# Norm and rotation of q and k: the squares in two buffers, the product with the cosines on VectorE

## The chip, the core and the metric

One NeuronCore of a Trainium2 chip runs the whole program; nothing is shared with other cores. The metric is the device time of one launch in microseconds (us), as the median of three runs. A core has engines with instruction queues of their own, each worked off in order: TensorE (PE in the rows; its weight loads are PEld), VectorE (DVE), ScalarE (ACT), GpSimd (POOL) and SyncE (SP), which here only issues transfers.

## The reference

One layer of a hybrid network on 1024 tokens of width 1024, all in float32: a feed-forward block, then a mixer of two branches (a recurrence, RWKV-7, and a dilated attention), then a second feed-forward block and a gated embedding. The change touches the attention's preparation of q and k:

```python
def rms_norm(x, gain):
    y = x * lax.rsqrt(jnp.mean(x * x, axis=-1, keepdims=True) + RMS_EPS)
    return y * gain
def apply_rope(x, cos, sin):
    x1, x2 = jnp.split(x, 2, axis=-1)
    return jnp.concatenate([x1 * cos - x2 * sin, x2 * cos + x1 * sin], axis=-1)
def dilated_attention_mix(z, cos, sin, q_gain, k_gain):
    q, k, v = jnp.split(z, 3, axis=-1)          # 12 heads of 64, in three groups of 4
    q = apply_rope(rms_norm(q, q_gain), cos, sin)
    k = apply_rope(rms_norm(k, k_gain), cos, sin)
    for gi, (window, dilation) in enumerate(((128, 1), (512, 4), (2048, 16))):
        ...   # banded causal attention of the group's 4 heads, with the log-sum-exp of each row
    ...       # the three groups' outputs, weighted by a softmax over their log-sum-exps
```

## The kernel before

Products of float32 matrices are made from split operands: a number is a rounded high part and a low part, and `mm3` issues three matmuls (L266 to L268) for each product. A weight tile is loaded by SyncE (L258), ScalarE writes its high part (L250) and GpSimd its low part (L251, tile `wsp`).

After the recurrence, from about 1387 us of the span to 1700, several streams are woven into one program:

- `qkv_gemm` makes q, k and v of groups 1 and 2 (g = 1, 2), 128 tokens at a time, in a PSUM tile `g` (two buffers) that ScalarE copies to `raw` (L1433). Group 0 was made earlier and is read back from memory into the tiles `ot` (L1491, two buffers). A gate product (L1352) shares the `g` buffers.
- `qk_post` is the norm and rotation. It runs 12 times: three groups, and in each q and k for two halves of 512 tokens (n = 0 to 3). Each time ScalarE squares the 128x1024 tile (L1510, into `rt2`), VectorE sums the squares over the 64 columns of a head (L1513), makes one over the root with eleven instructions on 128x16 numbers (L238 to L244), and rotates: a product with the cosines (L1512, into `rt1`, two buffers), two half products with the sines (L1519, L1520, into `rt3`), their sum (L1524) and the scaling (L1526). TensorE then transposes the result (L1531) and ScalarE copies it to `qkT`. Before the change GpSimd makes the product with the cosines, and `rt2` has one buffer, so a second square waits until L1513 has read the first.
- `attn_core` goes through eight blocks of queries in each group: scores on TensorE (L1591, tile `s`), mask and maximum on VectorE (L1595, then L1599), exponentials on ScalarE (L1601), transposes (L1613), copies (L1615 on VectorE, L1617 on ScalarE), and the product with v (L1634).
- `branch_r` is the recurrence's output product, which fills TensorE where the others leave room.

The order in which an engine's instructions stand is not the text's order: the streams yield at marked places with estimated times, and the layer that records the program places each engine's instructions by estimates of its own. Once built, an engine's order is fixed, and an instruction that waits holds back all that stand behind it. In the rows digits are left out of a tile's name: `rt1`, `rt2` and `rt3` all read `rt` there.

Of the kernel before, what the change touches and what calls it, by code (L numbers as in the profile page):

```python
# [13 lines left out]
ALU = mybir.AluOpType  # L14
# [4 lines left out]
P = 128  # L19
# [152 lines left out]
class K:  # L172
# [1307 lines left out]
    def qk_post(self, sp, sp1, pp, rawD, env):  # L1480

        nc = self.nc
        V, A, G, PE = nc.vector, nc.scalar, nc.gpsimd, nc.tensor
        done = env["done"]
        for g in range(NG):
            yield lambda: g < 2 or ("core", g - 2) in done
            tr = [self.t(sp, [P, 2, T], f"qkT{qk}", bufs=2) for qk in range(2)]

            def load0(n):
                t = self.t(sp1, [P, T], f"ot{n % 2}").rearrange("p (i h d) -> p i h d", i=4, h=4)  # L1490
                nc.sync.dma_start(t.rearrange("p i h d -> p i (h d)"), rawD[n % 2, :, n // 2 * 4:n // 2 * 4 + 4])  # L1491
                return t

            if g == 0:
                r0 = [load0(0), load0(1)]
                yield 0, 6.0
            for n in range(4):
                qk, hf = (n % 2, n // 2) if g == 0 else (n // 2, n % 2)
                Ct, St = self.rt[qk]
                if g == 0:  # L1500
                    raw = r0[n]
                else:
                    yield lambda: (g, qk, hf) in env["raw"]
                    raw = env["raw"][g, qk, hf]
                yield 0, 0.6
                isl = slice(hf * 4, hf * 4 + 4)
                bc = lambda t, o, n: t[:, isl, None, o:o + n].to_broadcast([P, 4, 4, n])
                ss = self.t(self.hp, [P, 4, 4], "ass", bufs=2)
                sq = self.t(sp, [P, 4, 4, 64], "rt2")
                A.activation(sq, raw, AF.Square)  # L1510
                t1 = self.t(sp, [P, 4, 4, 64], "rt1", bufs=2)
                G.tensor_tensor(out=t1, in0=raw, in1=bc(Ct, 0, 64), op=ALU.mult)  # L1512
                V.tensor_reduce(out=ss, in_=sq, axis=AX.X, op=ALU.add)  # L1513
                V.tensor_scalar(out=ss, in0=ss, scalar1=1.0 / 64, scalar2=1e-6, op0=ALU.mult, op1=ALU.add)
                yield 0, 1.5
                rs = self.rsqrt(sp, ss, "ars")
                yield 0, 1.0
                t2 = self.t(sp, [P, 4, 4, 64], "rt3")
                V.tensor_tensor(out=t2[:, :, :, 0:32], in0=raw[:, :, :, 32:64], in1=bc(St, 0, 32), op=ALU.mult)  # L1519
                V.tensor_tensor(out=t2[:, :, :, 32:64], in0=raw[:, :, :, 0:32], in1=bc(St, 32, 32), op=ALU.mult)  # L1520
                if g == 0 and n < 2:
                    r0.append(load0(n + 2))
                yield 0, 1.0
                V.tensor_tensor(out=t1, in0=t1, in1=t2, op=ALU.add)  # L1524
                yield 0, 1.0
                V.tensor_tensor(out=t1, in0=t1, in1=rs[:, :, :, None].to_broadcast([P, 4, 4, 64]), op=ALU.mult)  # L1526
                yield 0, 5.0
                for pr in range(2):
                    ps = self.t(pp, [P, HALF], "pt", bufs=2)
                    for i in range(4):  # L1530
                        PE.transpose(ps[:, i * P:(i + 1) * P], t1[:, i, 2 * pr:2 * pr + 2].rearrange("p h d -> p (h d)"),  # L1531
                                     self.ident)
                    t = tr[qk][:, pr]
                    if g == 0:
                        A.activation(t[:, hf * HALF:(hf + 1) * HALF], ps, AF.Copy)
                    elif g == 1:
                        A.activation(t.rearrange("p (r h l) -> p r h l", r=4, h=2)[:, :, hf],
                                     ps.rearrange("p (l r) -> p r l", r=4), AF.Copy)
                    else:
                        A.activation(t.rearrange("p (j h m) -> p j h m", j=8, h=2)[:, :, hf],  # L1540
                                     ps.rearrange("p (m j) -> p j m", j=8), AF.Copy)
                    yield 0.43, 0
                done.add(("post", g, qk, hf))
                env["qk"][g] = tr
# [569 lines left out]
```

## Time and profile before

| | |
|---|---|
| runs | 2688.59, 2697.83, 2698.99 us; median 2697.83 |
| profiled execution | 2694.29 us, its span (first to last instruction) 2692.5 |
| busy, share of the span | TensorE 93%, VectorE 60%, GpSimd 42%, ScalarE 36% |
| mean granted clock of TensorE | 0.964 of full speed |

The span is the time that the rows count from its start. Busy shares are averages over stages that have different limits; the rows further down are taken from the stage that the change touches. The chain of work that ended last runs 46% of the span through TensorE and 12% through VectorE.

### The profile page before, as it was taken

The page shows a single profiled execution, that of the slowest core. Times are in us where ns is not written, and L with a number is a line of the kernel's source. Part 1 is how long each engine was busy: PE and PEld are TensorE (multiplying, and loading weights), DVE is VectorE, ACT ScalarE, POOL GpSimd, SP SyncE. Part 2 cuts the span into 40 slices and gives each one's busy share as a digit, 9 for nine tenths or more (in the row PEclk, how much of TensorE's full clock was granted, in tenths as well). Part 3 has the DMA queues.
Part 4 walks back from the last instruction along what each step waited for, and adds up shares of the span by engine and source line. Part 5 has one row for each costly group of instructions (what it writes and reads, how often), then busy time and mean ns, then how long its engine had stood idle before and what let it go on. Part 6 is the DMA issues. An engine that isn't in the chain of part 4 may idle for free.

```text
span 2692.5 us, 36600 instructions
## 1 busy us (share of the span) xinstructions
PE 2492.6 (93%) x14285; PEld 2040.2 (76%) x14285; DVE 1623.3 (60%) x2591; ACT 977.2 (36%) x1700; POOL 1142.7 (42%) x637
## 2 busy tenths in 40 slices
PE   6899999899899999999989999879799999999889
PEld 5688888677787677779876988558578888778677
DVE  5855555898724565555456345462775556698952
ACT  6333333334444333333324354222533333333441
POOL 3675555544525233332222121240666555554540
PEclk9899999999999999999997999889899999999999
DMA  5322222646343222222231012661132222463432
GB/s 197 94 89 68 94 79 94 229 165 204 115 142 88 61 77 70 71 69 69 77 125 32 32 48 87 174 227 55 55 102 82 75 89 84 156 231 120 160 118 92
DMA packets 272497, 289.16 MB, mean 107 GB/s; under 512 B 46282, under 2 KB 202540, under 8 KB 272068
## 3 DMA queue, kind: packets, MB, share of 16 engines
q1 hardware_dynamic: 264932, 274.59, 31.2%
q10 hardware_dynamic: 7392, 12.23, 1.3%
q8 instruction: 112, 1.84, 0.3%
q14 instruction: 61, 0.50, 0.1%
HBM read 222.64 MB, written 64.14 MB: 107 GB/s over the span
## 4 chain that ended last, share of the span: by engine, by line
PE 46%; DVE 12%; issue 4%; POOL 3%; DMA 3%; ACT 2%; SPq 0%; DVEq 0%; POOLq 0%; ACTq 0%
PE g L266 7%; PE g L268 6%; PE g L267 6%; PE dn L267 5%; PE dn L268 5%; PE dn L266 5%; POOL wsp L251 2%; PE tr L268 1%; PE tr L267 1%; PE tr L266 1%; DVE X L1126 1%; DVE sub L1124 1%; PE s L1591 1%; PE t L1060 1%; DMA wr<-ffn_w_down 1%
## 5 line engine op out<-in xcount | busy, mean ns | idle before, releaser
L251 POOL TENSOR_TENSOR wsp<-wr,wsp 128x1024 fp32r<-128x1024 f32 (+1 forms) x158 | 356.6, 2263 | 378.8 <-ACT wsp L250 338.5
L251 POOL TENSOR_TENSOR wsp<-wst,wsp 128x1024 fp32r<-128x1024 f32 x71 | 176.1, 2483 | 344.9 <-ACT wsp L250 189.3
L251 POOL TENSOR_TENSOR wsp<-ws,wsp 128x1024 fp32r<-128x1024 f32 x88 | 221.1, 2514 | 214.5 <-ACT wsp L250 212.0
L266 PE MATMUL g<-wsp,h 128*128 128x256 f32 (+1 forms) x664 | 213.9, 322 | 19.5 <-ACT raw L1433 9.8
L266 PE MATMUL g<-h,wsp 128*128 128x512 f32 x496 | 215.9, 435 | 13.6 <-DVE h L1730 8.6
L268 PE MATMUL g<-wsp,h 128*128 128x256 f32 (+1 forms) x664 | 207.1, 312 | 0.0
L267 PE MATMUL g<-wsp,h 128*128 128x256 f32 (+1 forms) x664 | 206.0, 310 | 0.7 <-POOL wsp L251 0.7
L268 PE MATMUL g<-h,wsp 128*128 128x512 f32 x496 | 200.6, 405 | 2.1 <-POOL wsp L251 2.1
L267 PE MATMUL g<-h,wsp 128*128 128x512 f32 x496 | 200.6, 404 | 0.0
L408 DVE TENSOR_TENSOR ws<-wr 128x512 f32<-128x512 f32 x56 | 86.3, 1550 | 171.8 <-POOL x L251 170.4
L250 ACT ACTIVATE wsp<-wr 128x1024 fp32r<-128x1024 f32 (+1 forms) x158 | 134.3, 853 | 134.4 <-PE g L268 63.4
L250 ACT ACTIVATE wsp<-ws 128x1024 fp32r<-128x1024 f32 (+1 forms) x110 | 106.4, 968 | 202.1 <-PE dn L268 78.4
L266 PEld LDWEIGHTS g<-wsp,h 128*128 128x128 f32 x664 | 137.0, 206 | 29.6 <-ACT raw L1433 10.7
L266 PE MATMUL dn<-wsp,h 128*128 128x512 f32 x360 | 144.3, 402 | 6.5 <-DVE x L793 6.4
L267 PE MATMUL dn<-wsp,h 128*128 128x512 f32 x360 | 144.0, 400 | 6.5 <-POOL wsp L251 6.5
L268 PE MATMUL dn<-wsp,h 128*128 128x512 f32 x360 | 143.1, 399 | 0.8 <-DVE h L251 0.6
L267 PEld LDWEIGHTS g<-wsp,h 128*128 128x128 f32 x664 | 136.9, 206 | 4.9 <-POOL wsp L251 0.9
L268 PEld LDWEIGHTS g<-wsp,h 128*128 128x128 f32 x664 | 136.9, 206 | 4.6 <-issue 1.0
L464 DVE TENSOR_TENSOR act<-act,m 128x512 f32<-128x512 f32 x88 | 129.3, 1469 | 1.4
L266 PEld LDWEIGHTS g<-h,wsp 128*128 128x128 f32 x496 | 96.4, 194 | 38.5 <-DVE h L1730 9.5
L268 PE MATMUL dn<-h,wsp 128*128 128x512 f32 x320 | 124.6, 389 | 0.0
L266 PE MATMUL dn<-h,wsp 128*128 128x512 f32 x320 | 124.5, 389 | 0.0
(469 smaller groups left out, 6673.5 us busy)
## 6 DMA issues: line engine op xcount, KB each, us to landing
wr<-ffn_w_down SPq DMA_DIRECT2D x44, 1024.0 KB
wst<-w_in SPq DMA_DIRECT2D x60, 512.0 KB
wr<-ffn_w_gate SPq DMA_DIRECT2D x44, 512.0 KB
wr<-ffn_w_up SPq DMA_DIRECT2D x44, 512.0 KB
actD<-act SPq DMA_DIRECT2D x44, 512.0 KB
a<-actD SPq DMA_DIRECT2D x12, 1024.0 KB
gate<-gst SPq DMA_DIRECT2D x26, 256.0 KB
wst<-ffn_w_down SPq DMA_DIRECT2D x10, 512.0 KB
```

What stands on the lines that cost most here:

```text
L250: nc.scalar.activation(dst[:, 0], src, AF.Copy)
L251: (lo_eng or nc.vector).tensor_tensor(out=dst[:, 1], in0=src, in1=dst[:, 0].bitcast(F32), op=ALU.subtract)
L266: mm(ps, lhsT=l[0], rhs=r[0], start=first, stop=False)
L267: mm(ps, lhsT=l[0], rhs=r[1], start=False, stop=False)
L268: mm(ps, lhsT=l[1], rhs=r[0], start=False, stop=last)
L408: self.nc.vector.tensor_tensor(out=out, in0=R[:, i], in1=R[:, j], op=op)
L464: eng.tensor_tensor(out=a, in0=a, in1=v, op=ALU.mult)
L1060: PE.matmul(psd[h][:, i2, e].rearrange("p (a s) -> p a s", a=2), lhsT=BK[hr, i, 2 * e:2 * e + 2].rearrange("p a s -> p (a s)"), rhs=QR[hr, ...
L1124: V.tensor_tensor(out=pr[:, :s + 1, :n], in0=XT[:, :s + 1, s:s + 1].to_broadcast([64, s + 1, n]), in1=at[:, s:s + 1, s + 1:].to_broadcast( ...
L1126: V.tensor_tensor(out=XT[:, :s + 1, s + 1:], in0=XT[:, :s + 1, s + 1:], in1=pr[:, :s + 1, :n], op=ALU.subtract)
L1591: PE.matmul(ps[h][:, pr, :nk * P], lhsT=qT[hr, pr, j * P:(j + 1) * P], rhs=kT[hr, pr, k0:k0 + nk * P], start=True, stop=True)
```

## The change

Two lines of `qk_post` change. The squares get a second buffer, and the product with the cosines is issued on VectorE:

```diff
                 ss = self.t(self.hp, [P, 4, 4], "ass", bufs=2)
-                sq = self.t(sp, [P, 4, 4, 64], "rt2")
+                sq = self.t(sp, [P, 4, 4, 64], "rt2", bufs=2)
                 A.activation(sq, raw, AF.Square)
                 t1 = self.t(sp, [P, 4, 4, 64], "rt1", bufs=2)
-                G.tensor_tensor(out=t1, in0=raw, in1=bc(Ct, 0, 64), op=ALU.mult)
+                V.tensor_tensor(out=t1, in0=raw, in1=bc(Ct, 0, 64), op=ALU.mult)
                 V.tensor_reduce(out=ss, in_=sq, axis=AX.X, op=ALU.add)
```

GpSimd loses 12 instructions, VectorE gains 12; SyncE's order is the same as before. Around them the order on TensorE, VectorE and ScalarE shifts between the end of the recurrence and the norm of the last tile. Three places follow, as differences (+ only now, - only before).

ScalarE at the start of the attention: the squares of group 0's four tiles (rt 1842, 1857, 1877, 1910 for n = 0 to 3), the copies of `raw`, the gate's copy and a weight's high part.

```order
 L1510 ACTIVATE rt_1842_11915<-ot_1831_11828 128x1024
+L1510 ACTIVATE rt_1857_12073<-ot_1832_11830 128x1024
 L1352 ACTIVATE gst_1819_11776<-g_11777 128x512
 L250 ACTIVATE wsp_12129<-wst_12127 128x1024
-L1510 ACTIVATE rt_1857_12073<-ot_1832_11830 128x1024
+L1510 ACTIVATE rt_1877_12207<-ot_1848_11970 128x1024
 L1433 ACTIVATE raw_11842<-g_11869 128x256
-L1510 ACTIVATE rt_1877_12207<-ot_1848_11970 128x1024
 L1433 ACTIVATE raw_11842<-g_11895 128x256
```

The second square now stands directly behind the first, ahead of the gate's copy (L1352). The third stands ahead of both copies of `raw` (L1433); before, the first of these stood between the second square and the third.

VectorE at the same place: rt 1843 and 1858 are the products with the cosines for n = 0 and 1, rt 1847 and 1861 those with the sines, rt 1842 and 1857 the squares.

```order
+L1512 TENSOR_TENSOR rt_1843_11917<-ot_1831_11828,rope_1824_11816 128x1024
 L1519 TENSOR_TENSOR rt_1847_11967<-ot_1831_11828,rope_1825_11817 128x16x32
 L1520 TENSOR_TENSOR rt_1847_11967<-ot_1831_11828,rope_1825_11817 128x16x32
+L1512 TENSOR_TENSOR rt_1858_12075<-ot_1832_11830,rope_1826_11820 128x1024
 L1524 TENSOR_TENSOR rt_1843_11917<-rt_1843_11917,rt_1847_11967 128x1024
 L1519 TENSOR_TENSOR rt_1861_12117<-ot_1832_11830,rope_1827_11821 128x16x32
+L1513 TENSOR_REDUCE ass_11914<-rt_1842_11915 128x16
+L1513 TENSOR_REDUCE ass_12072<-rt_1857_12073 128x16
+L1514 TENSOR_SCALAR ass_11914<-ass_11914 128x16
 L1520 TENSOR_TENSOR rt_1861_12117<-ot_1832_11830,rope_1827_11821 128x16x32
+L238 TENSOR_SCALAR arsy_11941<-ass_11914 128x16
+L1514 TENSOR_SCALAR ass_12072<-ass_12072 128x16
```

Both products stand in VectorE's line, and the sums of squares of n = 0 and n = 1 (L1513) follow behind one L1524; before, the first stood behind both.

VectorE in the middle of group 0's attention: rt 1927 and 1964 are the products for the first two tiles of group 1, and S 12413 is the fifth block of scores of group 0.

```order
+L1512 TENSOR_TENSOR rt_1927_12447<-raw_11842,rope_1824_11816 128x1024
 L1524 TENSOR_TENSOR rt_1927_12447<-rt_1927_12447,rt_1939_12504 128x1024
+L1615 COPY PT_12363<-pt_12370 128x512
 L1526 TENSOR_TENSOR rt_1927_12447<-rt_1927_12447,arsy_12481 128x1024
-L1615 COPY PT_12363<-pt_12370 128x512
+L1512 TENSOR_TENSOR rt_1964_12637<-raw_11972,rope_1824_11816 128x1024
+L1595 ISA S_12413,ast_12185<-s_12414,cst_a_11814 128x256
+L1595 ISA ast_12185 128x1
```

The two products stand ahead of the mask and maximum of a block of scores, and each waits there for transposes (L1531) that free its buffer of `rt1`, as GpSimd waited before.

## Rows read from the trace of the kernel before

**Rows 1.** Busy time by stage: attention's start, and what follows.
```profile
core 0: us, PE busy (x) PEld busy (x) DVE busy (x) ACT busy (x) POOL busy (x), PEclk, DMA share, GB/s
1387.00:1480.00 93.00, 77.23 (x450) 59.10 (x449) 69.62 (x174) 37.21 (x93) 27.96 (x10) 0.80 0.18 60
1480.00:1560.00 80.00, 79.93 (x493) 76.72 (x492) 28.55 (x69) 24.95 (x59) 13.22 (x5) 1.00 0.08 27
```

**Rows 2.** TensorE's timeline, rows that waited (idle time and releaser in brackets).
```profile
1401.52 0.58 PE L266 MATMUL g<-wsp,h 128*128 128x256 f32 x1 [9.36 <-ACT raw L1433]
...
1433.37 1.13 PE L1591 MATMUL s<-qkT,qkT 64*128 64x256 f32 x6 [1.51 <-DVE ast L1595]
...
1435.54 0.48 PE L1613 MATMUL pt<-cst_p,S 128*128 128x128 f32 x1 [1.04 <-ACT S L1601]
...
1462.37 2.76 PE L1591 MATMUL s<-qkT,qkT 64*128 64x256 f32 x8 [2.28 <-DVE ast L1595]
...
1593.18 0.44 PE L1613 MATMUL pt<-cst_p,S 128*128 128x128 f32 x2 [1.99 <-ACT S L1601]
...
1618.55 1.94 PE L1531 MATMUL pt<-cst_p,rt 128*128 128x128 f32 x8 [5.93 <-DVE rt L1526]
```

**Rows 3.** Busy time in stretches of 2 us, columns as in Rows 1.
```profile
1434.00:1436.00 2.00, 0.96 (x7) 0.34 (x4) 2.00 (x5) 1.01 (x5) 0.00 (x0) 0.83 0.02 6
...
1462.00:1464.00 2.00, 1.63 (x6) 1.43 (x7) 2.00 (x8) 0.00 (x0) 0.00 (x0) 0.66 0.00 0
...
1476.00:1478.00 2.00, 2.00 (x14) 1.33 (x12) 0.77 (x2) 0.90 (x2) 0.00 (x0) 0.93 0.00 0
...
1592.00:1594.00 2.00, 0.82 (x7) 0.81 (x8) 1.76 (x10) 1.48 (x6) 0.00 (x0) 1.00 0.00 0
```

**Rows 4.** VectorE's timeline in the first stall (start, duration, instruction).
```profile
1388.12 2.87 DVE L1520 TENSOR_TENSOR rt<-ot,rope 128x512 f32<-128x512 f32 x1
...
1391.10 3.21 DVE L1524 TENSOR_TENSOR rt<-rt,rt 128x1024 f32<-128x1024 f32 x1
...
1394.34 2.71 DVE L1519 TENSOR_TENSOR rt<-ot,rope 128x512 f32<-128x512 f32 x1
...
1398.90 1.21 DVE L1513 TENSOR_REDUCE ass<-rt 128x16 f32<-128x1024 f32 x1
```

**Rows 5.** ScalarE's and GpSimd's timelines in the first stall.
```profile
1400.14 1.06 ACT L1510 ACTIVATE rt<-ot 128x1024 f32<-128x1024 f32 x1 [10.21 <-DVE ass L1513]
...
1387.55 5.67 POOL L1512 TENSOR_TENSOR rt<-ot,rope 128x1024 f32<-128x1024 f32 x2 [13.69 <-DMA ot<-raw]
...
1393.19 3.31 POOL L251 TENSOR_TENSOR wsp<-wst,wsp 128x1024 fp32r<-128x1024 f32 x1
```

**Rows 6.** Lines of the norm: count, duration ns min/median/max, first and last start.
```profile
L1524 DVE TENSOR_TENSOR rt<-rt,rt x12: 1208/1224/3241, 1391.1 to 1643.3; 128x1024 f32<-128x1024 f32 x12
...
L1520 DVE TENSOR_TENSOR rt<-raw,rope x8: 677/2870/2896, 1435.5 to 1640.3; 128x512 f32<-128x512 f32 x8
...
L1513 DVE TENSOR_REDUCE ass<-rt x12: 1205/1208/1212, 1398.9 to 1646.4; 128x16 f32<-128x1024 f32 x12
...
L1512 POOL TENSOR_TENSOR rt<-raw,rope x8: 2391/2848/2912, 1453.1 to 1639.8; 128x1024 f32<-128x1024 f32 x8
```

**Rows 7.** VectorE's timeline ahead of the wait that ends at 1462.37.
```profile
1455.54 1.23 DVE L1524 TENSOR_TENSOR rt<-rt,rt 128x1024 f32<-128x1024 f32 x1 [3.90 <-POOL rt L1512]
...
1458.54 1.73 DVE L238 TENSOR_SCALAR arsy<-ass 128x16 int32<-128x16 int32 x1
```

**Rows 8.** VectorE's and GpSimd's timelines ahead of the wait that ends at 1618.55.
```profile
1605.08 2.26 DVE L1519 TENSOR_TENSOR rt<-raw,rope 128x512 f32<-128x512 f32 x1 [8.56 <-ACT raw L1433]
...
1610.27 3.24 DVE L1524 TENSOR_TENSOR rt<-rt,rt 128x1024 f32<-128x1024 f32 x1
...
1604.41 2.39 POOL L251 TENSOR_TENSOR wsp<-wst,wsp 128x1024 fp32r<-128x1024 f32 x1 [16.27 <-ACT wsp L250]
```

**Rows 9.** Waits, all engines, 1380 to 1760: total us, times, longest.
```profile
POOL rt L1512 <- PE pt L1531: 36.4, 4, 19.4
```

## The prediction

> **What bounds the kernel now.** I began with the busy time by stage. From 1480 to 1560 us TensorE is busy for 79.93 of 80 us at full clock; from 1387 to 1480 it is busy for 77.23 of 93 at a mean clock of 0.80, while VectorE is at 69.62 [rows 1]. The change works from 1387 on, so what it can give lies where TensorE waits. Next I read TensorE's timeline for rows with idle time ahead of them. Six carry 22.11 us, and each names ScalarE or VectorE as its releaser, on instructions of the norm or on ones queued behind them [rows 2]. A stage that keeps TensorE full passes an earlier start on: if the first 90 us get shorter, the full stretch behind them starts earlier by as much.
>
> Third, the clock, in stretches of 2 us. It falls inside 1434 to 1436 (mean 0.83), behind two waits of 1.51 and 1.04 us, and inside 1462 to 1464 (0.66), behind one of 2.28. It did not fall in 1592 to 1594 (1.00), behind 1.99 [rows 2, 3]. The lower of the two levels is 1.2 GHz, the upper 2.4. A mean of 0.66 puts the fall at 1462.64, and the 0.93 of 1476 to 1478 the return at 1476.28: 13.6 us at half clock behind one wait of 2.28.
>
> Last, what holds VectorE. In the first stall L1520 took 2.87 us, L1524 3.21 and L1519 2.71 [rows 4]; the same lines take 0.68 and 1.21 at their shortest, and the median of L1520 on `raw` is 2.87, four times its shortest [rows 6]. L1513, with one input, took 1.205 to 1.212 us all twelve times [rows 6]. Beside the stretched ones GpSimd ran two products L1512 (5.67 us for both) and a split L251 [rows 5]. So an instruction of VectorE with two inputs waits out a GpSimd instruction that is under way: 0.68 and what is left of a product of some 2.4 make the 2.87 seen.
>
> **The change, step by step.** Twelve products leave GpSimd at 2.39 to 2.91 us each [rows 6]. VectorE gains twelve of the size of L1524, which takes 1.22 us by its median [rows 6]: 14.6 us of new work. Where it ran an instruction beside such a product, it loses up to 2.2 us of waiting for 1.2 of work; so I count the new work as hidden, and at its full 14.6 where that cover is missing.
>
> *First stall, 9.36 us until 1401.52.* Now: ScalarE's second square waits 10.21 us until L1513 has read the first one's only buffer, and TensorE's `g` waits behind it for the copy of `raw` [rows 2, 5]. After: the second square has a buffer, but the third needs the first back and stands ahead of that copy, so the stall ends one L1513 and one square later, not at once. Counted from the arrival of the data at 1387.55 [rows 5], VectorE's line up to the first L1513 is: product 1.22, L1519 and L1520 0.68 each, product 1.22, L1524 1.22, L1519 0.68, L1513 1.21, together 6.91, hence 1394.46. The weight split still on GpSimd will hold one of them by up to 2.4: 1396.86. Before, this L1513 ended at 1400.11 and TensorE went on 1.41 later [rows 2, 4]; after, at 1398.27. That is 3.2 us. Bounds: 5.7 without the split's hold; 0 if the third square's own load, which is asked for only when the first tile is free, lands as late as the stall ends now. I take 3.2, since that load is asked for some 1 us earlier than now. The gate's copy now stands one square later (1.06 [rows 5]), in a time in which TensorE goes on to wait anyway.
>
> *1.51 and 1.04 us near 1434.* VectorE's mask stood behind work stretched by a product. A product stays in its line there, and I count 0.8 (0 to 2.55).
>
> *2.28 us until 1462.37.* VectorE's L1524 waited 3.90 us for GpSimd's product, and L238, on no more than 128x16 numbers, took 1.73 beside the next product [rows 7]. After, the two products stand in VectorE's line, directly ahead of the mask that TensorE waits for, with one scaling between them instead of the row of stretched work. I take 2.3 (0 to 2.3).
>
> *1.99 us until 1593.18.* From the arrival of `raw`, L1519 (0.68), L1520 (2.87 beside a product) and L1513 (1.21) stood ahead of the mask [rows 6], 4.76 in all. In the new order the product (1.22) and L1513 do, 2.43, and the sines come behind. That is more than the wait; I take 1.9 (0 to 2.0).
>
> *5.93 us until 1618.55.* It ends a line of VectorE that starts with `raw` at 1605.08 and in which L1524 ends at 1613.51 [rows 8]; GpSimd runs three instructions beside it, one of them the product. Without it: the new product ends 1.22 behind the split that began at 1604.41 and takes 2.39 [rows 8], at 1608.02; L1519 waits for the second split, 2.39 + 0.68, 1611.09; L1520 and L1524 end at 1612.99. The rest of the line is as before. I take 0.5 (0 to 4.6, where no split intervenes: 1605.08 + 3.8 = 1608.88).
>
> *The clock.* With 2.28 us gone, the fall at 1462.64 has no wait ahead of it. The 13.6 us at half clock were filled with matmuls [rows 3]; at full clock they need 6.8 less, if nothing else holds them. ScalarE's exponentials will hold some, so I take 5 (0 to 6.8). For the fall near 1435 I count nothing: a wait of about 2 us is left there, and 1.99 did not lower the clock but 2.28 did.
>
> The sum is 3.2 + 0.8 + 2.3 + 1.9 + 0.5 + 5 = 13.7. Against the profiled execution's own 2694.29 us that is 2680.6. The median of the runs is 3.5 above that execution, so I forecast 2684.
>
> **A rule against it.** VectorE's two-input work is stretched beside GpSimd, its one-input L1513 never [rows 6]. The Trainium skill says of this, in Perfetto Trace Analysis, section Optimizing Scalar/DVE Operations, that GpSimd and VectorE share a read port, so that moving operations between the two might not help. By that rule the sum would be nothing instead of 13.7; the trace agrees on the sharing, and no run here shows yet what moving costs.
>
> **The rivals.**
> - *Moving gives nothing.* The weight splits stay on GpSimd and hold VectorE as the products did; then L1513 in the first stall ends where it ended, the third square waits for it in the second's place, and all waits stay. Against it: at 1462 no split stands near. Time 2694.3 + 3.5 = 2698, chance 0.26. (It is also what the rule above would give.)
> - *The products become the wait.* Now GpSimd waits four times, 36.4 us together, until L1531 has freed `rt1` [rows 9]. VectorE will wait in its place, and the mask L1595 of the running group is queued behind it, for which TensorE waits. It decides from the point where more than the 13.7 lies on the path; with all twelve products on it and none of the savings the time is 2694.3 + 14.6 + 3.5 = 2712. Against it: the transposes stand ahead of the scores on TensorE already, so the wait mostly ends before the mask could start. Chance 0.09.
> - *The clock stays up twice.* If the fall near 1435 goes as well, with another 5: 2694.3 - 18.7 + 3.5 = 2679. Against it: the wait that is left. Chance 0.15.
>
> **How the numbers follow.** My forecast has 0.50, with a range of its own from 2680 to 2690. A measurement of this kernel tells 0.5% from no change, 13.5 us; the boundary is 2684.3, and the forecast lies on it. I put 0.30 of its chance below and 0.20 above. Faster: 0.30 + 0.15 = 0.45. Same: 0.20 + 0.26 = 0.46. Slower: 0.09. The range of 2674 to 2700 leaves out the products' rival and the lowest end of the unknown costs (all at their upper bounds: 23.9 off, 2674 with the median's 3.5), some 2 in 10 together.
>
> **What would show it.** L1519, L1520 and L1524 near 0.68 and 1.22 wherever no split runs; L1513 unchanged. TensorE's wait near 1401 down to some 6 us; the one near 1462 gone, and the clock at 1.00 behind it; the one near 1593 gone; the one near 1618 still above 4. GpSimd without waits for L1531, VectorE with them but short. Wrong would be: VectorE's L1512 waiting for L1531 with TensorE then waiting for L1595; new waits of TensorE for ScalarE where the clock stays high; or an end of the stage, near 1700, that doesn't move although the waits are gone.

## The result

The median falls from 2696.81 us (four runs, 2688.59 to 2698.99) to 2673.35 (four runs, 2668.03 to 2677.97): ratio 0.9915, 95% interval 0.9894 to 0.9936. The profiled execution took 2668.03 us, with a span of 2666.2 and a mean granted clock of 0.971. The forecast was 2684 with a range from 2674; the time lies 0.65 us below its low end. Further down, the medians leave out two executions far off the others of their kernel (7557.77 us in e5 and 3456.52 in e8, slow runs).

Busy time by stage of the changed kernel, as in [rows 1]:

```profile
1387.00:1480.00 93.00, 85.93 (x599) 69.92 (x600) 69.97 (x188) 46.12 (x115) 11.23 (x4) 0.96 0.20 68
1480.00:1560.00 80.00, 80.00 (x496) 75.61 (x495) 28.44 (x92) 26.84 (x76) 10.43 (x4) 1.00 0.09 27
```

TensorE is now busy for 85.93 of the 93 us, at a mean clock of 0.96 instead of 0.80. Its timeline, rows that waited, as in [rows 2]:

```profile
1390.13 0.58 PE L266 MATMUL g<-wsp,h 128*128 128x256 f32 x1 [3.49 <-ACT gst L1352]
1396.79 0.45 PE L266 MATMUL g<-wsp,h 128*128 128x256 f32 x1 [2.03 <-ACT raw L1433]
1428.18 0.33 PE L1613 MATMUL pt<-cst_p,S 128*128 128x128 f32 x1 [1.22 <-ACT S L1601]
1433.95 0.93 PE L1613 MATMUL pt<-cst_p,S 128*128 128x128 f32 x4 [0.50 <-ACT S L1601]
1597.18 1.94 PE L1531 MATMUL pt<-cst_p,rt 128*128 128x128 f32 x8 [4.37 <-DVE rt L1526]
```

The waits that stood at 1462 and 1593 are gone; that of 9.36 is 2.03, behind one of 3.49 for the gate's copy (1.46 before); that of 5.93 is 4.37. The clock, in stretches as in [rows 3]:

```profile
1402.00:1480.00 78.00, 76.10 (x547) 60.28 (x546) 55.24 (x163) 40.28 (x108) 8.63 (x3) 1.00 0.13 42
1434.00:1436.00 2.00, 1.94 (x9) 1.04 (x10) 1.72 (x11) 1.38 (x6) 0.00 (x0) 1.00 0.80 239
1462.00:1464.00 2.00, 2.00 (x13) 1.35 (x12) 0.96 (x4) 0.60 (x1) 0.00 (x0) 1.00 0.00 0
```

It stays at its full level from 1402 to 1480. Both half-clock stretches, that behind 1435 and that behind 1462, are gone. The forecast had counted on one. Two more falls stand in the stage, and the forecast has no term for them: one in the first wait (10.2 us at half clock before, 6.8 after) and one at the wait of L1531 for L1526 (6.8 in both).

VectorE's timeline in the first wait, and below it GpSimd's, as in [rows 4, 5]:

```profile
1386.77 1.22 DVE L1512 TENSOR_TENSOR rt<-ot,rope 128x1024 f32<-128x1024 f32 x1 [16.68 <-DMA ot<-raw]
1387.91 0.68 DVE L1519 TENSOR_TENSOR rt<-ot,rope 128x512 f32<-128x512 f32 x1
...
1390.25 1.22 DVE L1524 TENSOR_TENSOR rt<-rt,rt 128x1024 f32<-128x1024 f32 x1
1391.50 2.75 DVE L1519 TENSOR_TENSOR rt<-ot,rope 128x512 f32<-128x512 f32 x1
1394.17 2.33 DVE L1513 TENSOR_REDUCE ass<-rt 128x16 f32<-128x1024 f32 x2
...
1391.10 2.60 POOL L251 TENSOR_TENSOR wsp<-wst,wsp 128x1024 fp32r<-128x1024 f32 x1 [18.02 <-ACT wsp L250]
```

The lines run at 1.22 and 0.68 us until a weight split of GpSimd starts at 1391.10; the L1519 beside it takes 2.75. By lines, over all instructions (count, duration in ns min/median/max), as in [rows 6]:

```profile
L1524 DVE TENSOR_TENSOR rt<-rt,rt x12: 1206/1222/1225, 1390.2 to 1623.4; 128x1024 f32<-128x1024 f32 x12
L1520 DVE TENSOR_TENSOR rt<-raw,rope x8: 678/684/687, 1429.4 to 1621.7; 128x512 f32<-128x512 f32 x8
L1512 DVE TENSOR_TENSOR rt<-raw,rope x8: 1215/1226/2803, 1443.0 to 1616.1; 128x1024 f32<-128x1024 f32 x8
```

L1524 and L1520 are at their shortest throughout, where their longest were 3.24 and 2.90 us before. The new product takes 1.2 us, and 2.80 beside a split.

**Where the time came from.** The instant at which the stage of the change begins varies by 9 us between the profiled executions of this study, for reasons ahead of the change. So I measure from the start of the last transpose of the recurrence (L1335 on TensorE), and cut the stage at the starts of four kinds of instruction: the first transpose of rotated q and k (L1531), the first transpose of probabilities (L1613), the first transpose of group 0's statistics (L1569, with which that group ends), the last copy of `raw` (L1433), and the last L1569, with which the attention ends. All lengths in us, each the difference of two starts:

| kernel | to L1531 | to L1613 | to L1569 | to last `raw` | to last L1569 | stage | ratio to before [95%] |
|---|---|---|---|---|---|---|---|
| before | 36.0 | 20.7 | 50.9 | 151.3 | 61.0 | 319.9 | 1 |
| the change | 31.9 | 18.3 | 41.3 | 146.2 | 60.5 | 298.2 | 0.9915 [0.9894, 0.9936] |
| e1 second buffer alone | 35.5 | 20.7 | 51.3 | 151.2 | 60.9 | 319.6 | 0.9997 [0.9982, 1.0011] |
| e2 product alone | 32.0 | 18.4 | 41.9 | 145.8 | 60.9 | 299.0 | 0.9916 [0.9898, 0.9935] |
| e3 change + unread product on GpSimd | 38.5 | 22.9 | 44.2 | 148.7 | 61.1 | 315.4 | 0.9979 [0.9967, 0.9992] |
| e4 change, three buffers | 29.1 | 20.2 | 43.5 | 145.6 | 61.0 | 299.4 | 0.9934 [0.9908, 0.9960] |
| e5 change + unread copy on GpSimd | 34.9 | 19.8 | 46.2 | 147.1 | 60.6 | 308.6 | 0.9941 [0.9919, 0.9964] |
| e6 change + 12 splits on VectorE | 31.9 | 16.9 | 41.4 | 139.8 | 59.9 | 289.9 | 0.9883 [0.9866, 0.9899] |
| e7 = e6, three buffers | 28.9 | 18.0 | 42.2 | 139.9 | 59.8 | 288.8 | 0.9899 [0.9882, 0.9916] |
| e8 before + 12 splits on VectorE | 37.1 | 18.6 | 41.2 | 147.8 | 59.5 | 304.2 | 0.9950 [0.9929, 0.9971] |
| e9 change, product moved in group 0 only | 30.9 | 18.3 | 49.2 | 150.0 | 60.7 | 309.1 | 0.9971 [0.9956, 0.9986] |
| e10 change, product moved in groups 1, 2 only | 35.5 | 20.7 | 43.9 | 147.4 | 60.7 | 308.2 | 0.9959 [0.9944, 0.9975] |
| e11 = e6 + the last gate's split on VectorE | 28.9 | 17.7 | 41.4 | 139.9 | 60.0 | 287.9 | 0.9862 [0.9846, 0.9877] |

The stage holds the same 1997 matmuls in the kernel before and in the change, but the parts don't: between the first L1613 and the first L1569 stand 276 before and 293 in the change. Six of these 17 are scores (L1591) that stood ahead of the first L1613, and eleven are of the products made by `mm3` (L266 to L268) and stood behind the first L1569. So the middle columns are to be read together with the number of matmuls.

The change gains 21.7 us in the stage: 4.1, 2.4, 9.6, 5.1 and 0.5. The spans differ by 26.3; 0.8 of it lies ahead of the stage and 3.8 behind it, where no instruction of the change stands.

### The profile page after: what moved, and what is told of

It is laid out like the page before. It is cut to its first block, busy times and chain, and to the rows that moved or that the text cites. A ratio compares the mean times of both kernels' runs of the same rounds, so it can differ in the third digit from the quotient of the medians.

```text
span 2666.2 us, 36580 instructions
## 1 busy us (share of the span) xinstructions
PE 2481.7 (93%) x14285; PEld 2034.9 (76%) x14285; DVE 1613.7 (61%) x2603; ACT 977.2 (37%) x1700; POOL 1109.9 (42%) x625
## 4 chain that ended last, share of the span: by engine, by line
PE 46%; DVE 12%; issue 3%; DMA 3%; POOL 3%; ACT 2%; SPq 0%; DVEq 0%; POOLq 0%; ACTq 0%
PE g L266 7%; PE g L268 6%; PE g L267 6%; PE dn L267 5%; PE dn L268 5%; PE dn L266 5%; POOL wsp L251 2%; PE tr L267 1%; PE tr L266 1%; PE tr L268 1%; DVE X L1126 1%; PE s L1591 1%; DVE sub L1124 1%; PE t L1060 1%; PE po L1634 1%
## 5 line engine op out<-in xcount | busy, mean ns | idle before, releaser
L266 PE MATMUL g<-h,wsp 128*128 128x512 f32 x496 | 216.4, 436 | 11.8 <-DVE h L1730 7.2
L266 PE MATMUL g<-wsp,h 128*128 128x256 f32 (+1 forms) x664 | 215.0, 324 | 8.0 <-ACT gst L1352 3.5
L268 PE MATMUL g<-wsp,h 128*128 128x256 f32 (+1 forms) x664 | 207.3, 312 | 0.0
L268 PE MATMUL g<-h,wsp 128*128 128x512 f32 x496 | 200.6, 405 | 2.1 <-POOL wsp L251 2.1
L266 PE MATMUL dn<-wsp,h 128*128 128x512 f32 x360 | 143.7, 400 | 9.8 <-DVE x L793 5.8
L266 PEld LDWEIGHTS g<-wsp,h 128*128 128x128 f32 x664 | 137.6, 207 | 18.8 <-issue 4.1
L268 PE MATMUL dn<-wsp,h 128*128 128x512 f32 x360 | 142.0, 396 | 0.1
L268 PEld LDWEIGHTS g<-wsp,h 128*128 128x128 f32 x664 | 137.8, 208 | 4.0 <-issue 0.3
L268 PE MATMUL dn<-h,wsp 128*128 128x512 f32 x320 | 124.8, 390 | 0.0
L267 PE MATMUL tr<-h,wsp 128*128 128x512 f32 x320 | 124.6, 389 | 0.0
L266 PE MATMUL dn<-h,wsp 128*128 128x512 f32 x320 | 124.6, 389 | 0.0
```

The costliest lines, as they stand in the source:

```text
L266: mm(ps, lhsT=l[0], rhs=r[0], start=first, stop=False)
L267: mm(ps, lhsT=l[0], rhs=r[1], start=False, stop=False)
L268: mm(ps, lhsT=l[1], rhs=r[0], start=False, stop=last)
```

## The experiments

My theory after the result: the gain is the product's leaving GpSimd, which had held VectorE's two-input instructions; waits of TensorE got shorter, and with them two falls of the clock went. Rivals: the second buffer alone; the wait of L1524 for GpSimd's product rather than the holding; GpSimd's load as a whole. In the rows of the kernels with an inserted line, line numbers behind it are one higher.

**e1 and e2: the two halves of the change.** e1 puts the product back, e2 takes the second buffer away:

```diff
 e1
-                V.tensor_tensor(out=t1, in0=raw, in1=bc(Ct, 0, 64), op=ALU.mult)
+                G.tensor_tensor(out=t1, in0=raw, in1=bc(Ct, 0, 64), op=ALU.mult)
 e2
-                sq = self.t(sp, [P, 4, 4, 64], "rt2", bufs=2)
+                sq = self.t(sp, [P, 4, 4, 64], "rt2")
```

> The change with its product back on GpSimd: only the second square buffer is left. My theory: the gain comes from taking the product off GpSimd, which stretched VectorE's two-input instructions from 0.68 to 2.87 us and held L1524; the waits of TensorE of about 1.5 and 2.3 us near 1434 and 1462 us come back, and the two half-clock stretches of about 13 us with them. Time within 5 us of the kernel before, about 2694; L1520 on raw near 2.87 us again. Rival, the buffer alone does it: the time is that of the change, about 2673, and the first long wait of TensorE is as short as in the change (3.5 + 2.0 us).

> The change with one square buffer: only the product is moved to VectorE. My theory: the first long wait of TensorE comes back in part, 3 to 4 us longer than in the change, and all else stays: about 2676, and no half-clock stretch between 1402 and 1480 us. Rival, the buffer does it: about 2694 to 2697.

e1 took 2695.9 us beside 2698.13 before; e2 took 2676.12. TensorE's waits in e1:

```profile
1440.96 1.13 PE L1591 MATMUL s<-qkT,qkT 64*128 64x256 f32 x6 [1.52 <-DVE ast L1595]
1470.13 2.76 PE L1591 MATMUL s<-qkT,qkT 64*128 64x256 f32 x8 [2.28 <-DVE ast L1595]
```

The waits of 1.5 and 2.28 us are back, with the durations of [rows 2]; the second buffer is worth 0.5 us by the stage (36.0 to 35.5 at L1531). e2 has the change's stage to within 0.8 us. I had expected its first wait to return by 3 to 4 us: its two rows (1.54 and 5.49 us) are 1.5 us longer together than the change's, and the start of L1531 moved by only 0.1. The buffer theory is out: the product alone is the gain.

**e3: a product that nobody reads.** GpSimd makes the product as before, into a tile of its own, and VectorE makes its own as in the change. The order on TensorE, VectorE and ScalarE is that of the change.

```diff
                 V.tensor_tensor(out=t1, in0=raw, in1=bc(Ct, 0, 64), op=ALU.mult)
+                G.tensor_tensor(out=self.t(sp, [P, 4, 4, 64], "rtg"), in0=raw, in1=bc(Ct, 0, 64), op=ALU.mult)
```

> The change, and beside it a copy of the product made by GpSimd into a tile that nobody reads: VectorE does not wait for a product of GpSimd, but GpSimd runs as many instructions beside VectorE's as before. If the stretching of VectorE's two-input instructions was the cost (my theory), most of the gain is lost: 2688 to 2700, with L1520 on raw above 2 us and at least one of the two half-clock stretches back. Rival, the cost was only that L1524 waited for GpSimd's product to be ready: the time stays at about 2673 to 2678.

2692.1 us: three quarters of the gain are lost. VectorE's timeline in and behind the first wait, GpSimd's, and TensorE's two longest waits of the first group:

```profile
1389.92 1.23 DVE L1512 TENSOR_TENSOR rt<-ot,rope 128x1024 f32<-128x1024 f32 x1 [16.56 <-DMA ot<-raw]
1391.06 2.84 DVE L1520 TENSOR_TENSOR rt<-ot,rope 128x512 f32<-128x512 f32 x1
1393.82 2.86 DVE L1521 TENSOR_TENSOR rt<-ot,rope 128x512 f32<-128x512 f32 x1
...
1406.16 0.16 DVE L1515 TENSOR_SCALAR ass<-ass 128x16 f32<-128x16 f32 x1
...
1414.88 2.37 DVE L1515 TENSOR_SCALAR ass<-ass 128x16 f32<-128x16 f32 x1
...
1389.98 6.15 POOL L1513 TENSOR_TENSOR rtg<-ot,rope 128x1024 f32<-128x1024 f32 x2 [13.63 <-DMA ot<-raw]
...
1406.52 0.58 PE L266 MATMUL g<-wsp,h 128*128 128x256 f32 x1 [8.56 <-ACT raw L1433]
...
1442.67 0.48 PE L1614 MATMUL pt<-cst_p,S 128*128 128x128 f32 x1 [5.81 <-ACT S L1602]
```

Nobody waits for this product, and yet the sines (L1520, L1521 here) take 2.84 and 2.86 us instead of 0.68, and TensorE waits 8.56 us again. So the holding is most of the cost; neither the wait of L1524 for its input nor a shifted order of instructions is in this kernel, whose order is the change's. The other 4.5 us of the stage (319.9 less 315.4) are not divided between those two.

Not only instructions with two inputs are held: L1515, which scales 128x16 numbers and has one, took 2.37 us beside a product of GpSimd that runs from 1413.96 for 3.26 us, and 0.16 alone. L238 in [rows 7] is another of this kind.

**e4: three buffers.** The third square then has a buffer too (`bufs=3`).

> The change with three square buffers in place of two. In the change the first long wait still stands as 3.5 + 2.0 us of TensorE near 1390 and 1397, the last of them behind a square that waits for its buffer. If the third square's buffer is what is left of that wait, 0 to 2 us go: 2671 to 2673. If the arrival of the data ends it, nothing changes: 2673. Both are inside what the measurement can tell apart in the time, so the wait near 1397 in the profile decides.

2682.81 us, where 2671 to 2673 were expected; the interval overlaps the change's. The start of L1531 comes 2.8 us sooner (29.1 against 31.9), and a wait of TensorE for the first probabilities gives it back:

```profile
1433.52 0.33 PE L1613 MATMUL pt<-cst_p,S 128*128 128x128 f32 x1 [3.18 <-ACT S L1601]
```

The stage ends as in the change (299.4 and 298.2). Its profiled execution reached the stage 6.2 us later (L1335 at 1384.2 against 1378.0), which is no work of the buffers.

**The clock's share.** TensorE has the same order of instructions in the change, e2, e3, e4 and e5 (which follows), and the clock fell in different ways behind the first probabilities. Their stretch from the first L1613 to the first L1569, in that order of kernels:

```profile
1428.18:1469.45 41.27, 40.59 (x293) 28.69 (x293) 28.82 (x102) 26.12 (x82) 2.37 (x1) 1.00 0.06 20
...
1435.51:1477.40 41.89, 41.77 (x293) 29.69 (x293) 28.73 (x102) 26.09 (x82) 2.36 (x1) 0.96 0.06 20
...
1442.67:1486.90 44.23, 44.10 (x293) 30.73 (x293) 28.30 (x102) 26.24 (x82) 2.35 (x1) 0.90 0.06 19
...
1433.52:1477.00 43.48, 43.35 (x294) 30.22 (x295) 28.30 (x102) 26.28 (x82) 2.34 (x1) 0.92 0.06 19
...
1440.66:1486.90 46.24, 46.12 (x293) 31.90 (x293) 28.30 (x102) 26.12 (x82) 2.36 (x1) 0.85 0.05 18
```

At a mean clock of 1.00 the same matmuls take 40.59 us; at 0.96, 0.92, 0.90 and 0.85 they take 41.77, 43.35, 44.10 and 46.12. e5 has one half-clock stretch of 13.7 us here, as long as each of the two before, and it costs 5.5 us (46.12 less 40.59). In the kernel before the mean was 0.73 and the stretch 50.9 us. So part of the 9.6 us of this stretch is a clock that no longer falls; how much falls to which wait is told by e9 and e10.

**e5: a copy instead of the product.** As e3, with one input:

```diff
+                G.tensor_copy(self.t(sp, [P, 4, 4, 64], "rtg"), raw)
```

> As the run with the unread product of GpSimd, but GpSimd copies raw into the tile that nobody reads, with one input in place of two. If any GpSimd instruction holds VectorE's two-input ones, the time stays near that run's 2692 and L1520 (one line lower here) is stretched above 2 us in the first wait. If only GpSimd's two-input instructions hold them (my theory: in the trace each stretched one lies beside a product, a split or a sum of GpSimd, all with two inputs), the time is near that of the change, 2673 to 2679, and L1520 is at 0.68 beside the copies.

2683.27 us; by the stage, half of the gain is lost (308.6 us, between 298.2 and 319.9), and my theory was wrong here. GpSimd's and VectorE's timelines:

```profile
1394.69 3.53 POOL L1513 COPY rtg<-ot 128x1024 f32<-128x1024 f32 x2 [13.61 <-DMA ot<-raw]
...
1403.16 1.04 POOL L1513 COPY rtg<-ot 128x1024 f32<-128x1024 f32 x1 [1.04 <-DMA ot<-raw]
...
1395.80 1.52 DVE L1520 TENSOR_TENSOR rt<-ot,rope 128x512 f32<-128x512 f32 x1
1397.24 1.52 DVE L1521 TENSOR_TENSOR rt<-ot,rope 128x512 f32<-128x512 f32 x1
```

A copy of 1.04 us holds the sines too, for a shorter time: 1.52 us instead of 0.68. So what counts here is that GpSimd has an instruction under way, and how long it runs.

**e6, e7 and e8: the weight splits too.** In the change what still holds VectorE are the splits. e6 is the change with the splits of groups 1 and 2 made by VectorE, e7 is e6 with three square buffers, e8 is the kernel before with this edit alone:

```diff
-        self.split(sp[:, :, :n], st[:, :n], lo_eng=nc.gpsimd)
+        self.split(sp[:, :, :n], st[:, :n], lo_eng=lo or nc.gpsimd)
...
         return [self.wchunk(self.a["w_in"][b * 512:(b + 1) * 512, c0:c0 + 256].rearrange("(k p) n -> p k n", p=P), 4,
+                            lo=self.nc.vector if g else None)
```

> The change, and the twelve weight splits L251 of the second and third group made by VectorE instead of GpSimd. In the change a split of 2.60 us stretches one L1519 of the first wait to 2.75, and two of 5.73 stretch L1512 and L1519 to 2.80 and 2.89 ahead of TensorE's wait of 4.37 us near 1597. My theory (what counts is what stands in VectorE's line): the two splits then take some 1.2 us each in the same line, so that the wait near 1597 falls by about 1.3 us and the one near 1397 by up to 2: 2669 to 2674, at most 5 below the change. Rival (each instruction taken off GpSimd gains as the products did): 20 us for twelve, about 2653. Second rival (VectorE's line gets too long for the mask): slower than the change by up to 12 times 1.2, 2688.

> Both at once: three square buffers and the splits on VectorE. With three buffers alone the first wait was 2.8 us shorter by the start of the first transposes, and a wait of 3.18 us for the first probabilities gave it back, since VectorE's line ahead of the mask had not become shorter. With the split out of the first wait that line starts earlier: if so, 2666 to 2671. If the splits, standing in the same line, cost what they free, it is as the change, 2673 to 2680.

> The kernel before (product on GpSimd, one square buffer) with only the twelve splits moved to VectorE. It tells whether taking any work off GpSimd in this stage brings the gain. My theory: the products still stretch L1519, L1520 and L1524, both half-clock stretches stay, the time is 2690 to 2700. Rival, the load on GpSimd as a whole was the cost: 2680 or less.

e6 took 2663.58 us (2669 to 2674 expected), e7 2668.51 and e8 2681.84, beside 2696.26 before. TensorE's waits in e6, and the line of VectorE that is still held, with what holds it:

```profile
1397.88 0.58 PE L266 MATMUL g<-wsp,h 128*128 128x256 f32 x1 [2.05 <-ACT raw L1434]
1593.90 1.06 PE L1532 MATMUL pt<-cst_p,rt 128*128 128x128 f32 x8 [0.59 <-DVE rt L1527]
...
1392.48 2.86 DVE L1520 TENSOR_TENSOR rt<-ot,rope 128x512 f32<-128x512 f32 x1
...
1392.42 2.38 POOL L251 TENSOR_TENSOR wsp<-wst,wsp 128x1024 fp32r<-128x1024 f32 x1 [45.63 <-ACT wsp L250]
```

The wait of 4.37 us near 1597 is down to 0.59, not by the 1.3 that I had expected. The clock stays up behind it, and the part of the stage up to the last `raw` is 6.4 us shorter. The wait near 1397 stays, since the split in it is that of a gate's weights, not one of the twelve. e7 is not told apart from e6. e8 gains 14.4 us by the median, against my theory, which gave it nothing: moving the splits alone gave about three quarters of what moving the products gave (15.7 us of the stage against e2's 20.9). Both moves together gain 30.0 (319.9 to 289.9), less than the sum of 36.6, since they take away in part the same waits.

e8 also shows a wait of TensorE nearly as long as that of 2.28 us before, without a fall of the clock behind it, and the wait of 1.99 us with one, where the clock stayed up before [rows 3]:

```profile
1461.35 1.81 PE L1592 MATMUL s<-qkT,qkT 64*128 64x256 f32 x8 [2.20 <-DVE ast L1596]
...
1462.00:1476.00 14.00, 13.76 (x98) 9.25 (x98) 9.95 (x40) 8.06 (x28) 0.00 (x0) 1.00 0.01 2
...
1586.76 0.62 PE L1614 MATMUL pt<-cst_p,S 128*128 128x128 f32 x2 [1.99 <-ACT S L1602]
...
1588.00:1590.00 2.00, 2.00 (x12) 2.00 (x11) 1.45 (x4) 0.42 (x3) 0.00 (x0) 0.50 0.00 0
```

**e9 and e10: group by group.**

```diff
 e9
+                (V if g == 0 else G).tensor_tensor(out=t1, in0=raw, in1=bc(Ct, 0, 64), op=ALU.mult)
 e10
+                (G if g == 0 else V).tensor_tensor(out=t1, in0=raw, in1=bc(Ct, 0, 64), op=ALU.mult)
```

> The change with VectorE making the product of the first group only (4 of 12); GpSimd makes the other eight. Where does the gain of the stage lie? If each half-clock stretch hangs on its own wait: the first wait and the waits near 1434 are as in the change (4.1 and 2.4 us less by the starts of the first transposes and the first probabilities), the first stretch is gone, and the wait of about 2.3 us near 1462 comes back with its stretch of 13 us: about 2686. If the second fall came only because the clock had fallen shortly before (with the splits alone moved, a wait of 2.20 us near 1461 lowered nothing): the wait near 1462 comes back without a stretch, about 2681. The two waits near 1593 and 1618 come back in both.

> The opposite: GpSimd makes the four products of the first group, VectorE the eight of the second and third. The first long wait stays at about 8 us, the waits near 1434 at 1.5 and 1.0 with the half-clock stretch behind them; the wait near 1462 is gone and with it the second stretch; the waits near 1593 and 1618 are as in the change. Gains of 2.3 and 4 near 1462 and 4 later: about 2687. If the products of the first group alone hold the stage, it is as the kernel before, 2697.

2688.12 and 2686.28 us, where 2686 and 2687 were expected with each stretch hanging on its own wait. First e9: its wait near 1458, and the clock ahead of it and behind. Then e10: the waits near 1438, and the clock behind them.

```profile
1457.90 2.34 PE L1591 MATMUL s<-qkT,qkT 64*128 64x256 f32 x7 [2.20 <-DVE ast L1595]
...
1406.00:1456.00 50.00, 47.78 (x327) 37.94 (x326) 41.57 (x113) 24.28 (x59) 13.97 (x5) 0.99 0.14 43
1458.00:1470.00 12.00, 12.00 (x46) 7.89 (x48) 6.82 (x35) 4.90 (x18) 0.00 (x0) 0.50 0.01 1
```

```profile
1437.58 1.13 PE L1591 MATMUL s<-qkT,qkT 64*128 64x256 f32 x6 [1.53 <-DVE ast L1595]
1439.75 0.39 PE L1613 MATMUL pt<-cst_p,S 128*128 128x128 f32 x1 [1.04 <-ACT S L1601]
...
1438.00:1452.00 14.00, 12.96 (x53) 7.32 (x52) 10.39 (x38) 7.69 (x27) 2.34 (x1) 0.57 0.14 44
1454.00:1484.00 30.00, 29.88 (x227) 22.04 (x224) 20.20 (x66) 18.45 (x55) 0.00 (x0) 1.00 0.00 1
```

Each has one of the two falls. What the falls cost is read from the stretch from the first L1613 to the first L1569, in e9, in e10 and in e8, where the clock stays up:

```profile
1433.83:1482.97 49.14, 46.21 (x292) 32.34 (x292) 28.27 (x101) 25.86 (x82) 7.68 (x3) 0.86 0.05 17
...
1439.75:1483.64 43.89, 43.77 (x280) 30.45 (x281) 28.75 (x101) 25.50 (x80) 2.34 (x1) 0.84 0.04 13
...
1439.75:1480.87 41.12, 38.46 (x283) 27.87 (x283) 26.94 (x101) 25.26 (x80) 5.28 (x2) 1.00 0.06 20
```

e9's is 7.9 us above the change's 41.3: the wait of 2.20, and half clock, which made TensorE's busy time 5.6 longer (46.21 against 40.59) with one matmul less. e10's is only 2.6 above, but thirteen fewer matmuls stand in it (280 against 293); e8 works off 283 in 38.46 us, so that e10's half clock cost 5.3 or somewhat more (43.77 less 38.46, by an order of instructions that differs a little). In group 0 the products cost the first wait and the first fall, in the later groups the second fall and the two late waits.

**e11: the last split.** e6, and in `gates` the split of the last block's weights on VectorE as well:

```diff
-            W = self.gate_w(b)
+            W = self.gate_w(b, None, "wsp", 3, self.nc.vector if b == 15 else None)
```

> The version with the twelve splits on VectorE, and with the one split of the last gate's weights on VectorE as well: it is the GpSimd instruction of 2.38 us beside which one L1519 of the first wait still took 2.86 us, with a wait of TensorE of 2.05 us behind it. The split takes about 1.2 us in VectorE's line in its place, so that 1 to 2 us of that wait go: 2661 to 2663, near or below what the measurement tells apart; the wait decides. If VectorE's line gets longer at the wrong place, the wait stays.

2658.45 us, ratio 0.9862 [0.9846, 0.9877]; against e6 the intervals overlap, but the profile is clear. The start of L1531 comes 3.0 us sooner. VectorE's line ahead of L1514 (L1513 before), without the stretch, and all that is left of the first wait on TensorE:

```profile
1392.41 0.69 DVE L1520 TENSOR_TENSOR rt<-ot,rope 128x512 f32<-128x512 f32 x1
1393.03 2.34 DVE L1514 TENSOR_REDUCE ass<-rt 128x16 f32<-128x1024 f32 x2
...
1391.50 0.58 PE L266 MATMUL g<-wsp,h 128*128 128x256 f32 x1 [3.45 <-ACT gst L1352]
```

The wait of about 2 us for `raw` is gone. Its median is the lowest of the kernels here.

## Why the prediction was right in its mechanism and too small

**What held, and what the runs added.** TensorE's waits set the stage, and a stage that gets shorter passes its lead on: the lead of 16.9 us at the end of group 0 (1486.4 to 1469.5) is 22.5 at the end of the attention. VectorE's two-input instructions, and L238 and L1515 with one, wait out a GpSimd instruction; e3 shows that this holding alone costs most of what the change gives. On GpSimd a product holds VectorE for as long as it runs, 2.39 us at the shortest [rows 6]; in VectorE's own line it takes 1.22. So the move also pays where the product stays in the line that matters.

**The terms.** They added up to 13.7 us; the stage gave 21.7. Of the 8.0 between them, some 5.5 are a term that stood at nothing.

- *First stall: 3.2 forecast, 4.1 measured.* The chain was as told: the third square waits for the first L1513, which a split holds up through one L1519 of 2.75 us. From the arrival of the data to the end of that L1513 I had 9.3 us; it was 8.6 (1386.77 to 1394.17 and 1.21 more). The second buffer, which I had put ahead, has little part in it (e1: 0.5; e2: 4.0 without it).
- *Near 1434: 0.8 forecast, 0.8 measured in waits.* The two left are 1.22 and 0.50 in place of 1.51 and 1.04. No row gave the 0.8, so that it fits is luck. The part is 2.4 us shorter, since the six scores, 1.13 us before [rows 2], now stand behind the first L1613.
- *Near 1462, with its fall of the clock: 2.3 + 5 forecast.* e9, which has both back, is 7.9 longer than the change: 2.20 and some 5.6. This term was right.
- *The fall near 1435: nothing forecast.* This is the step that failed: "a wait of about 2 us is left there, and 1.99 did not lower the clock but 2.28 did". The waits left were 1.22 and 0.50, and the clock did not fall; a stretch of that length costs 5.5 us by e5 and 5.3 or more by e10. Nor is there a limit between 1.99 and 2.28: 2.20 lowered the clock in e9 and did not in e8, and 1.99 did in e8. That the clock stays up near 1435 is not certain even with the change's order of instructions: in e2, with a wait of 1.32, it fell for 3.4 us. The rival "the clock stays up twice", at 0.15, is what happened.
- *Near 1593 and 1618: 1.9 + 0.5 forecast, 3.5 measured in waits.* The first wait went, as told. The second fell by 1.56 instead of 0.5: the splits held the product (2.80) and one L1519 (2.89), as told, but from `raw` to the end of L1524 it took 7.5 us (1584.66 to 1592.14) and not 7.9. The part up to the last `raw` is 5.1 us shorter, not 3.5, because eleven matmuls, at 0.23 us from one start to the next, now stand ahead of it.

With 5.5 for each fall, an estimate from e5, the terms are 4.1 + 0.8 + 2.3 + 5.5 + 5.5 + 3.5 = 21.7, the stage's gain.

**From the sum to the median.** I added 3.5 us, by which the median lay above the profiled execution of before; for the changed kernel it is 5.3 (2673.35 against 2668.03). The median of before less the stage's 21.7 is 2675, inside the range and 1.8 above what was measured. The interval of the ratio puts the changed kernel between 2668 and 2680, with the low end of 2674 in it, so on which side of that end the median fell is chance; that the gain was 8 us larger than the sum is not. The 3.8 us behind the stage can't be put down to the change, since that part varies as much between kernels that differ in nothing there (from the last L1569 to the last L1766: 103.1 before, 101.0 after, 103.5 in e1, 100.0 in e2).

**The rivals.** "Moving gives nothing" is out. The Trainium skill (Perfetto Trace Analysis, section Optimizing Scalar/DVE Operations) warns that moving operations between GpSimd and VectorE might not help; here moving the product alone gave a ratio of 0.9916, and moving the splits alone 0.9950. "The products become the wait" is out too: VectorE waited for L1531 once, for 1.6 us, and no wait of TensorE stood behind it.

## What to carry to other kernels

Where VectorE feeds the engine that sets the time, look at what GpSimd runs beside its instructions: the sign is the same line at a multiple of its shortest duration, and the cost is the length of GpSimd's instruction, even of one whose result nobody waits for. A move to VectorE then pays if the work is shorter there, and what else GpSimd runs in that stage is the next thing to move (e6, e11). Price a wait of TensorE together with the half-clock stretch behind it, which here cost more than the wait itself; and don't take a wait length from one trace as the limit from which the clock falls. Where two kernels are compared part by part, count the matmuls in each part first: a shifted order moves work from one part into the next.

## What the runs showed of the hardware that was not expected

- A one-input copy of GpSimd holds VectorE's two-input instructions as a product does, for about its own length: 0.68 becomes 1.52 us beside copies of 1.04, and 2.84 beside products of 2.34. GpSimd waits in turn: two products beside two sines took 6.15 us (2 x 2.34 + 2 x 0.68 = 6.04), two copies 3.53 (2 x 1.04 + 2 x 0.68 = 3.44). The Trainium skill says the same in SBUF — State Buffer, section 🔬 SBUF: two separate sides: the pair of ports is an exclusive lock for the whole instruction, between GpSimd and VectorE instructions that have two inputs from SBUF or run in a two-port mode. One-input L1513 was 1.20 to 1.21 us beside both, but one-input L1515 took 2.37 us in e3 instead of 0.16; no run shows in which mode it ran.
- A wait of 2.20 us lowered TensorE's clock in e9 and not in e8, both with the clock up ahead of it and TensorE busy for 96% of the 44 and 50 us before. A wait of 1.99 us lowered it in e8 and not before. What tells them apart stays open.
- A half-clock stretch of 13.7 us did not double the time of the work in it: it cost 5.5 us in e5 with the change's own order of matmuls, 5.6 in e9, and 5.3 or somewhat more in e10, where 6.8 would be half of the stretch.
